# Summing the adaLN modulation by quarters of the partitions in a one-core decoder layer

## The chip, the core and the metric

The kernel runs on one core of one Trainium2 chip. The metric is the device time of one execution in microseconds (us), from the first to the last instruction with what lies around them; lower is better.

## The reference

One layer over a sequence of 256 tokens with 2048 channels, batch 1, all in float32: a SwiGLU FFN (hidden width 5632), a mixer of two parallel branches (causal pooling and windowed attention), and a second SwiGLU FFN. Each of the three is modulated by a vector c of 2048 numbers:

```python
mod = (jax.nn.silu(c) @ w_ada[l] + b_ada[l]).reshape(B, 3 * N_SUB, 1, D)

h = modulate(rms_norm(x, g_ffn1[l]), mod[:, 0], mod[:, 1])
x = x + 0.5 * mod[:, 2] * swiglu(h, w_ffn1_gu[l], w_ffn1_down[l])
...
```

So there are nine modulation vectors of 2048 numbers. For each sub-layer i, vector 3i is a shift, 3i + 1 a scale and 3i + 2 a gate on the residual. w_ada is 2048 by 18432, 151 MB, 16.8 MB for each vector. The product with one row silu(c) has so little arithmetic per weight that the kernel gives it to VectorE.

## The kernel before

**The large products.** TensorE multiplies activations by weights in float32r. For accuracy both are split into a high part (ScalarE's cast, L285) and the rest (VectorE's subtraction, L289), and three products are added: hi by hi, lo by hi, hi by lo (`mm`, L292 to L304). A `Set` is a block of output columns, at most 1024 wide, over all slices k of 128 rows of a weight matrix; it holds four PSUM banks (two token tiles by two chunks of 512). One slice k of a set is one *turn*: 2 token tiles by 3 terms by 2 chunks, 12 matmuls of 128x128 by 512 columns. Weights come as tiles named raw of 1 MB, two slices at a time, by one DMA each on SP's queue (`load`, L258 to L262). There are six raw buffers, shared with the modulation's weights.

**The order.** It is written out by hand. `push` (L106) issues the splitting of a slice two turns ahead (LAG) of its matmuls; `at(n, f)` (L116) puts extra work into turn n; `hop(n, f, g)` (L124) puts a small product into turn n and its use into the next, away from the ends of sets. A planner keeps an account of VectorE's time per turn: `room` is what a turn has (ROOM, 2.6 us for a full turn), `busy` what is booked by `will(n, t)`; `spread(n0, m, cost, cap)` (L143) puts m pieces of work of a given cost into the first turns with room, at most `cap` us of them a turn. In the two FFN calls the cap is ROWS.

**The modulation.** Vectors 0 and 1 come first, on a path of their own (`ada_load`, `ada_acc`, `ada_col`, L650 to L672 and L804 to L823), which the change leaves as it is apart from the shape of its column of ones. The other seven go through `ada_plan` (L180 to L237). For a block of 1024 (or, twice for vector 7, 512) outputs, 16 slices of w_ada are loaded, each 128 rows on the 128 partitions; VectorE multiplies a slice by the 128 numbers of silu(c) that belong to it (cs, one per partition) and adds it to an accumulator acc (L228, L230). Then acc must be summed over the partitions, in chunks of 512 outputs (`sums`): acc is split in two float32r halves (L189, L190), TensorE multiplies both by a 128x128 matrix of ones (L195, L196), and every partition then has every sum. For a gate that is the form wanted, and ScalarE copies it to `gates` (L202). For a shift or scale the numbers are wanted in columns, channel by partition: `mod_col` multiplies by the identity (L168), reduces (L171), and adds the biases (L175 to L178).

**Which vectors run where.** Vectors 2, 4, 3 and the first 512 outputs of 7 run in the second half of the first FFN (the `ffn` call at L902); 5, 6 and the rest of 7 in the mixer (L1180); 8 in the second FFN (L1261). Gate 2 is used when the first FFN's output is added to x (L420), gate 5 in the mixer's output projection, gate 8 at the end.

**The mixer's attention** copies the outputs of two heads from PSUM with VectorE (L1166) and books 0.8 us for them. It loads its bias tables on POOL's queue (L1138).

Of the kernel before, what the change touches and what calls it, by code (L numbers as in the profile page):

```python
# [9 lines left out]
F32 = mybir.dt.float32  # L10
F32R = mybir.dt.float32r
# [5 lines left out]
P = 128  # L17
# [16 lines left out]
RAW = 6  # L34
# [2 lines left out]
NS = 7  # L37
LAG = 2
ROOM = 2.6
ROWS = 1.3  # L40


@with_exitstack
def trunk_layer(ctx, tc, x, c, w_ada, b_ada, g_ffn1, w_ffn1_gu, w_ffn1_down, g_mix, w_in,
# [10 lines left out]
    def nm(s):  # L55
        uid[0] += 1
        return f"{s}_{uid[0]}"

    def t_(shape, tag, bufs=1, dt=F32):
        return sb.tile(list(shape), dt, tag=tag, bufs=bufs, name=nm(tag))  # L60
# [16 lines left out]

    ident = const.tile([P, P], F32, name="ident")
    make_identity(nc, ident)
    ones_f = const.tile([P, P], F32, name="ones_f")  # L80
    nc.gpsimd.memset(ones_f, 1.0)
    ones = const.tile([P, P], F32R, name="ones")
    nc.vector.tensor_copy(ones, ones_f)

    x_sb = const.tile([P, T, D], F32, name="x_sb")

# [29 lines left out]
    def at(n, f, first=False):  # L116

        fs = plan.setdefault(max(n, done[0]), [])
        fs.insert(0, f) if first else fs.append(f)
# [35 lines left out]
    def will(n, t):  # L155
        busy[n] = busy.get(n, 0.0) + t

    ada_v = w_ada[0].rearrange("(k p) n -> p k n", p=P)  # L160
    mcol = const.tile([P, 9, KD], F32, name="mcol")
    gates = {}

    def mod_col(j, b, c0):

        k, n = c0 // P, b.shape[1] // P
        d = t_([P, n, P], "t2", T2)
        nc.vector.tensor_tensor(d, b.rearrange("p (a q) -> p a q", a=n),  # L168
                                ident.unsqueeze(1).to_broadcast([P, n, P]), ALU.mult)
        m = mcol[:, j, k:k + n]  # L170
        nc.vector.tensor_reduce(m, d, AX.X, ALU.add)  # L171
        i, o = j // 3, j % 3
        bc = bcol[:, (2 * i + o) * KD + k:(2 * i + o) * KD + k + n]
        if o == 0:
            nc.vector.tensor_tensor(m, m, bc, ALU.add)  # L175
        else:
            nc.vector.scalar_tensor_tensor(out=m, in0=m, scalar=1.0, in1=bc, op0=ALU.add, op1=ALU.add)
            nc.vector.tensor_tensor(m, m, gcol[:, i * KD + k:i * KD + k + n], ALU.mult)  # L178

    def ada_plan(js, n0, cap=9.0):  # L180

        def sums(j, c0, a, n, o):
            got = []

            def halves():
                hi, lo = t_([P, CW], "t2", T2, F32R), t_([P, CW], "t2", T2, F32R)
                nc.scalar.copy(hi, a[0][:, o:o + CW])  # L189
                nc.vector.tensor_tensor(lo, a[0][:, o:o + CW], hi.bitcast(F32), ALU.subtract)  # L190
                got.extend((hi, lo))

            def prod():
                got.append(bank())
                nc.tensor.matmul(got[2], ones, got[0], start=True, stop=False)  # L195
                nc.tensor.matmul(got[2], ones, got[1], start=False, stop=True)  # L196

            def use():
                if j % 3 == 2:
                    if j not in gates:  # L200
                        gates[j] = t_([P, D], "gate", 1)
                    nc.scalar.activation(gates[j][:, c0 + o:c0 + o + CW], got[2], AF.Copy, scale=1.0 if j == 5 else 0.5)  # L202
                else:
                    mod_col(j, got[2], c0 + o)

            at(n, halves)
            q = hop(n + 2, prod, use, 2)
            will(n, 0.65)
            if j % 3 != 2:
                will(q + 1, 1.7)  # L210
            return q

        for j, c0, a_w in js:
            a, r, nk = [], [], 2 * SW // a_w
            where = spread(n0, KD, 1.24 * a_w / SW, cap)
            for kk, n in enumerate(where):
                def go(j=j, c0=c0, kk=kk, a=a, r=r, w=a_w, nk=nk):
                    if kk == 0:
                        a.append(t_([P, w], "acc", 2))
                        if j % 3 == 2:  # L220
                            nc.gpsimd.memset(a[0], 0.0)
                            nc.gpsimd.dma_start(a[0][0:1, :], b_ada[0:1, j * D + c0:j * D + c0 + w])
                    if kk % nk == 0:
                        r[:] = [t_([P, nk, w], "raw", RAW)]
                        nc.sync.dma_start(r[0], ada_v[:, kk:kk + nk, j * D + c0:j * D + c0 + w])
                    sc = cs[:, kk:kk + 1]
                    if kk == 0 and j % 3 != 2:
                        nc.vector.tensor_scalar_mul(a[0], r[0][:, 0, :], sc)  # L228
                    else:
                        nc.vector.scalar_tensor_tensor(out=a[0], in0=r[0][:, kk % nk, :], scalar=sc, in1=a[0],  # L230
                                                       op0=ALU.mult, op1=ALU.add)
                at(n, go)
                will(n, 1.24 * a_w / SW)
            n0 = n
            q = n
            for i in range(a_w // CW):
                q = sums(j, c0, a, max(n + 1 + 2 * i, q + 1), i * CW)  # L237


    class Set:  # L240
# [406 lines left out]

    at(16, small_things)

    def ada_load(c0, w, k0):  # L650
        nk = SW // w
        raw = t_([P, nk, 2, w], "raw", RAW)
        for j in (1, 0):
            nc.sync.dma_start(raw[:, :, j, :], ada_v[:, k0:k0 + nk, j * D + c0:j * D + c0 + w])  # L654
        return raw
# [103 lines left out]
    for j in (1, 0):  # L759
        for kk in (13, 14, 15):  # L760
            ada_acc(acc0[:, j], braw[3][:, kk - 12, j], kk, False)
        first_pe(12, j)
        for a in range(2):
            nc.tensor.matmul(bsum[j][a], acc0[:, j, a * P:(a + 1) * P], ones_f[:, 0:1], start=False, stop=True)
        if j:
            b8 = x_T(xr[1], bank_at(6, (P, 2, S)))
    nc.vector.tensor_copy(gcol, b[:, :KG])
# [37 lines left out]
    for k, n, need in ((2, 4, 14), (6, 4, 42), (10, 4, 70), (14, 2, 74)):  # L805
        nk = SW // (n * P)
        acc, raw, cost = [], [], 1.28 * n / 4

        def rows(kk, k=k, n=n, nk=nk, acc=acc, raw=raw):
            if kk == 0:  # L810
                acc.append(t_([P, 2, n * P], "acc", 2))
            if kk % nk == 0:
                raw[:] = [ada_load(k * P, n * P, kk)]
            ada_acc(acc[0], raw[0][:, kk % nk], kk, kk == 0)

        def end(k=k, n=n, acc=acc):
            b = bank((P, 2, n))
            for j in (1, 0):
                for a in range(n):
                    nc.tensor.matmul(b[:, j, a:a + 1], acc[0][:, j, a * P:(a + 1) * P], ones_f[:, 0:1],  # L820
                                     start=True, stop=True)
            for j in (1, 0):
                ada_col(k, n, j, b[:, j, :])  # L823

        where = [kk * 12 // KD for kk in range(KD)] if k == 2 else spread(max(e, 14), KD, cost)
        for kk in range(KD):
            at(where[kk], lambda rows=rows, kk=kk: rows(kk))
            will(where[kk], cost)
        e = where[-1] + (2 if k > 6 else 1)
        assert e + 1 < need, (k, e, need)  # L830
        will(e, 0.4)
        will(e + 1, 0.65 * n // 2)
        at(e, end)

        q = k
        while q < k + n:
            m = 1 if q == k + n - 1 else 2
            if q - q % 2 in xT:
                at(e + (q > k + 1), lambda q=q, m=m: h_pair(xT[q - q % 2][:, q % 2:q % 2 + m, :], q, m))
            else:  # L840
                xn, o = [], (q - k) // 2
                at(e - 1 + o, lambda q=q, xn=xn, m=m: xn.append(x_row(q, m)))
                n_ = e + 1 + o
                while n_ in ends or n_ - 1 in ends:
                    n_ += 1
                at(n_, lambda q=q, xn=xn, m=m: h_pair(x_T(xn[0], bank((P, m, S))), q, m))
            q += m
# [47 lines left out]
    def toe_out():  # L895
# [4 lines left out]

    hop(pushed[0] + 8, toe_prod, toe_out)
    s = ffn(w_ffn1_gu[0], w_ffn1_down[0], hh, hl, actT, NS // 2 * SW, part[NS - 1], None, 2, sumsq,  # L902
            [(j, c, SW) for j in (2, 4, 3) for c in (0, SW)] + [(7, 0, CW)])


    WI = w_in[0]
# [177 lines left out]
    def heads(n, g):  # L1084
# [78 lines left out]

        for blk in range(2):
            with_bank(n + 8, (P, 2, P), out_prod(blk),
                      lambda b, blk=blk: nc.vector.tensor_copy(attnT[:, g - 1:g + 1, blk * P:(blk + 1) * P], b), 1)  # L1166
        will(n + 9, 0.8)

    for half_ in range(2):
        for q in range(2):  # L1170
# [6 lines left out]
        will(W1 - 1 + 2 * q, 1.4)  # L1177
    for g, n in enumerate((2, 5, 9, 13, 17, 22, 25, 28)):
        heads(G[0] + n, g)
    ada_plan([(j, c, SW) for j in (5, 6) for c in (0, SW)] + [(7, CW, CW), (7, SW, SW)], nQ)  # L1180

    tk = [(t, i) for t in range(T) for i in range(2)]

# [74 lines left out]

    g, hh, hl = transition(s, SW, 5, 6, lambda stat: Set(w_ffn2_gu[0], KD, (0, SW), stat, flip=False, late=True))
    actT = t_([P, KF, S], "big", 1)  # L1260
    s = ffn(w_ffn2_gu[0], w_ffn2_down[0], hh, hl, actT, 0, None, g, 8, store, [(8, 0, SW), (8, SW, SW)])  # L1261
    flush()
    items = last_items(s, *new_h())

# [71 lines left out]
```

## Time and profile before

| | |
|---|---|
| three runs | 1994.84 us median (1994.56 to 1996.48) |
| the profiled execution | 1996.08 us, its span 1994.3 us |
| TensorE clock granted | 0.996 of full speed |
| DMA | 523.68 MB, mean 263 GB/s |

Here is the span in 40 slices of 50 us. The first FFN runs to about 767 us, the mixer to about 1263 us, the second FFN to the end. Each digit is the busy share of a slice in tenths; GB/s is what the DMA engines moved.

```profile
DVE  6898867989999978886889998888455454565655
ACT  6543457664664546446656455645564645565443
DMA  9989745899899966876688996598555645466652
GB/s 364 371 314 342 261 164 187 329 337 356 313 363 336 335 230 235 310 281 219 235 292 302 351 311 219 212 356 317 214 189 202 219 170 190 159 225 216 218 185 74
```

The stages in which `ada_plan` works stand out: DVE (VectorE) and DMA are at 8 to 9 tenths from 350 to 700 us, again over most of 800 to 1250 us, and from 1300 to 1400 us; elsewhere DMA is at 5 or 6.

In the rows, PE is TensorE's matmuls, PEld its weight loads, ACT ScalarE, POOL GpSimd, SP SyncE, which issues most DMAs. A matmul's duration is longer than the time between two of them, since they overlap; the pace is read from the chain.

### The profile page before, as it was taken

The page shows a single profiled execution, that of the slowest core. Times are in us where ns is not written, and L with a number is a line of the kernel's source. Part 1 is how long each engine was busy: PE and PEld are TensorE (multiplying, and loading weights), DVE is VectorE, ACT ScalarE, POOL GpSimd, SP SyncE. Part 2 cuts the span into 40 slices and gives each one's busy share as a digit, 9 for nine tenths or more (in the row PEclk, how much of TensorE's full clock was granted, in tenths as well). Part 3 has the DMA queues.
Part 4 walks back from the last instruction along what each step waited for, and adds up shares of the span by engine and source line. Part 5 has one row for each costly group of instructions (what it writes and reads, how often), then busy time and mean ns, then how long its engine had stood idle before and what let it go on. Part 6 is the DMA issues. An engine that isn't in the chain of part 4 may idle for free.

```text
span 1994.3 us, 23770 instructions
## 1 busy us (share of the span) xinstructions
PE 1972.3 (99%) x8873; PEld 1629.3 (82%) x8873; DVE 1513.6 (76%) x1749; ACT 1091.8 (55%) x1484; POOL 26.4 (1%) x51
## 2 busy tenths in 40 slices
PE   7999999999999999999999999999999999999999
PEld 6788888888788888888788888888888888888887
DVE  6898867989999978886889998888455454565655
ACT  6543457664664546446656455645564645565443
POOL 0000000000000000000000000000000000000000
PEclk9999999999999999999999999999999999999999
DMA  9989745899899966876688996598555645466652
GB/s 364 371 314 342 261 164 187 329 337 356 313 363 336 335 230 235 310 281 219 235 292 302 351 311 219 212 356 317 214 189 202 219 170 190 159 225 216 218 185 74
DMA packets 158212, 523.68 MB, mean 263 GB/s; under 512 B 9325, under 2 KB 21509, under 8 KB 157840
## 3 DMA queue, kind: packets, MB, share of 16 engines
q1 hardware_dynamic: 156464, 518.83, 72.7%
q0 software_dynamic: 1632, 3.34, 0.6%
q8 instruction: 69, 1.13, 0.2%
q14 instruction: 47, 0.39, 0.1%
HBM read 520.00 MB, written 2.12 MB: 262 GB/s over the span
## 4 chain that ended last, share of the span: by engine, by line
PE 96%; DVE 2%; DMA 1%; SPq 0%; issue 0%; ACT 0%; DVEq 0%; ACTq 0%
PE bank L304 93%; DVE acc L662 1%; DMA raw<-in_w_ffn_gu_dram 1%; DMA raw<-in_w_ada_dram 0%; DVE wl L289 0%; PE bank L1065 0%; SPq L654 0%; PE bank L820 0%; PE bank L196 0%; PE bank L195 0%; PE bank L357 0%; PE bank L1128 0%; PE bank L1092 0%; PE bank L999 0%; PE bank L1051 0%
## 5 line engine op out<-in xcount | busy, mean ns | idle before, releaser
L285 ACT CAST wh<-raw 128x1024 fp32r<-128x1024 f32 (+2 forms) x711 | 711.1, 1002 | 793.9 <-PE bank L304 739.7
L289 DVE TENSOR_TENSOR wl<-raw,wh 128x1024 fp32r<-128x1024 f32 (+2 forms) x713 | 823.5, 1157 | 418.4 <-ACT wh L285 413.7
L304 PE MATMUL bank<-wh,hl 128*128 128x512 f32 (+1 forms) x2088 | 653.6, 388 | 0.0
L304 PE MATMUL bank<-wh,hh 128*128 128x512 f32 (+1 forms) x2064 | 651.3, 390 | 0.3 <-DVE big L1099 0.3
L304 PE MATMUL bank<-wl,hh 128*128 128x512 f32 (+1 forms) x2064 | 647.5, 389 | 0.6 <-DVE wl L289 0.6
L304 PEld LDWEIGHTS bank<-wh,hl 128*128 128x128 f32 x2088 | 392.7, 188 | 81.3
L304 PEld LDWEIGHTS bank<-wl,hh 128*128 128x128 f32 x2064 | 388.2, 188 | 82.9 <-DVE wl L289 2.9
L304 PEld LDWEIGHTS bank<-wh,hh 128*128 128x128 f32 x2064 | 386.4, 189 | 80.2 <-issue 0.8
L230 DVE SCALAR_TENSOR_TENSOR acc<-raw,cs,acc 128x1024 f32<-128x1024 f32 (+1 forms) x231 | 279.8, 1211 | 0.8
L304 PE MATMUL bank<-wh,sh 128*128 128x512 f32 x656 | 203.7, 390 | 0.0
L304 PE MATMUL bank<-wh,sl 128*128 128x512 f32 x656 | 203.3, 389 | 0.0
L304 PE MATMUL bank<-wl,sh 128*128 128x512 f32 x656 | 203.1, 389 | 0.0
L304 PEld LDWEIGHTS bank<-wh,sl 128*128 128x128 f32 x656 | 123.0, 188 | 26.0 <-DVE sl L394 0.3
L304 PEld LDWEIGHTS bank<-wl,sh 128*128 128x128 f32 x656 | 123.1, 188 | 25.8
L304 PEld LDWEIGHTS bank<-wh,sh 128*128 128x128 f32 x656 | 122.6, 188 | 25.8 <-issue 0.4
L542 ACT COPY big<-raw 32x512 f32<-32x512 f32 (+1 forms) x208 | 121.9, 586 | 4.2
L662 DVE SCALAR_TENSOR_TENSOR acc<-raw,cs,acc 128x1024 f32<-128x1024 f32 (+2 forms) x74 | 77.7, 1052 | 1.0
L394 DVE TENSOR_TENSOR sl<-big,sh 128x512 fp32r<-128x512 f32 x82 | 56.2, 686 | 0.0
L393 ACT CAST sh<-big 128x512 fp32r<-128x512 f32 x82 | 50.7, 618 | 0.0
L784 DVE TENSOR_TENSOR big<-bank,big 128x512 f32<-128x512 f32 x56 | 36.4, 684 | 0.0
L329 ACT ACTIVATE junk<-x_sb 128x512 bf16<-128x512 f32 x24 | 15.2, 632 | 13.9 <-DVE x_sb L421 11.7
L538 DVE STREAM_TRANSPOSE raw<-sg 128x1024 f32<-128x1024 f32 (+1 forms) x20 | 22.7, 1133 | 0.0
(220 smaller groups left out, 802.7 us busy)
## 6 DMA issues: line engine op xcount, KB each, us to landing
raw<-in_w_ffn_gu_dram SPq DMA_DIRECT2D x175, 1024.0 KB, 5.3
raw<-in_w_ada_dram SPq DMA_DIRECT2D x112, 1024.0 KB, 7.2
raw<-in_w_ffn_down_dram SPq DMA_DIRECT2D x86, 1024.0 KB, 6.1
raw<-in_w_in_dram SPq DMA_DIRECT2D x48, 1024.0 KB, 6.8
raw<-in_w_ada_dram SPq DMA_DIRECT2D x64, 512.0 KB, 7.6
raw<-in_w_o_dram SPq DMA_DIRECT2D x15, 1024.0 KB, 7.8
raw<-in_w_pool_up_dram SPq DMA_DIRECT2D x8, 1024.0 KB, 7.9
raw<-in_w_attn_up_dram SPq DMA_DIRECT2D x8, 1024.0 KB, 6.9
```

The source lines that it names most:

```text
L230: nc.vector.scalar_tensor_tensor(out=a[0], in0=r[0][:, kk % nk, :], scalar=sc, in1=a[0], op0=ALU.mult, op1=ALU.add)
L285: nc.scalar.copy(wh, raw_k)
L289: nc.vector.tensor_tensor(wl[:, e], raw_k[:, e], wh[:, e].bitcast(F32), ALU.subtract)
L304: nc.tensor.matmul(self.banks[t][i], a[:, sl], w[:, o], start=first and q == 0, stop=last and q == 2)
L329: nc.scalar.activation(junk, x_sb[:, t, n * CW:(n + 1) * CW], AF.Square, scale=(D / 2) ** -0.5, accum_out=ssq[:, t, n:n + 1])
L393: nc.scalar.copy(hi, src[:, k:k + n, :])
L394: nc.vector.tensor_tensor(lo, src[:, k:k + n, :], hi.bitcast(F32), ALU.subtract)
L538: nc.vector.transpose(z[0][:, t, :], (src() if callable(src) else src)[:, t, 0:n])
L542: nc.scalar.copy(actT[32 * j:32 * j + 32, k:k + m, :].rearrange("p k (t i r) -> p k t i r", t=T, i=4)[:, :, :, i, :], z[0][32 * i:32 * i + ...
L662: nc.vector.scalar_tensor_tensor(out=acc, in0=r, scalar=sc, in1=acc, op0=ALU.mult, op1=ALU.add)
L784: nc.vector.tensor_tensor(a, b, a, ALU.add)
```

## The change

- A new view of w_ada: a tile of 128 partitions now holds, in each quarter q of 32 partitions, 32 rows of w_ada for the outputs 512q to 512q + 511. One accumulator of 128x512 serves a whole vector of 2048 outputs. A vector takes 64 accumulations of 128x512 (one for each group of 32 rows) where it took 32 of 128x1024.
- A raw tile (four groups of 32 rows) is loaded by four DMAs of 256 KB, each to 32 partitions, in runs of 2 KB.
- silu(c) is laid out anew to match (cs4), by 16 small ScalarE copies between turns 80 and 92.
- Shifts and scales (4, 3, 7, 6): the accumulator's four 128x128 blocks are the float32 weights, and the moving operand is `ind`, four columns, column q being 1 on quarter q's partitions. The result is the vector in columns at once; there are no halves and no `mod_col`.
- Gates (2, 5, 8): the halves are taken once for the whole vector, multiplied with `ind` as the weights, which gives four rows of 512; these are scaled, written to DRAM on POOL's queue, and read back to all 128 partitions.
- The planner: 0.75 us a row of 512; ROWS is 1.5, not 1.3; vector 7 is split at 24 of 64 rows instead of at a quarter of its columns; in the mixer the rest of 7 comes first, then 5 and 6.
- The attention's output copies go to ScalarE, and their 0.8 us are no longer booked.

```diff
-ROWS = 1.3
+ROWS = 1.5
...
+    ind = const.tile([P, 4], F32, name="ind")
+    nc.gpsimd.memset(ind, 0.0)
+    for q in range(4):
+        nc.gpsimd.memset(ind[32 * q:32 * q + 32, q:q + 1], 1.0)
...
+    ada_q = w_ada[0].rearrange("(m r) n -> r m n", r=32)
...
+            def row_prod():
+                got.append(bank())
+                nc.tensor.matmul(got[2][0:4, :], indr, got[0], start=True, stop=False)
+                nc.tensor.matmul(got[2][0:4, :], indr, got[1], start=False, stop=True)
+
+            def row_use():
+                nc.scalar.activation(a[0][0:4, :], got[2][0:4, :], AF.Copy, scale=1.0 if j == 5 else 0.5)
+                row = dram.tile([1, D], F32, name=nm("row"))
+                nc.gpsimd.dma_start(row[0].rearrange("(q n) -> q n", q=4), a[0][0:4, :])
+                gates[j] = t_([P, D], "gate", 1)
+                nc.gpsimd.dma_start(gates[j], row[0:1, :].to_broadcast([P, D]))
+
+            def col_prod():
+                got.append(bank((P, 4, 4)))
+                for c_ in range(4):
+                    nc.tensor.matmul(got[0][:, c_, :], a[0][:, c_ * P:(c_ + 1) * P], ind, start=True, stop=True)
+
+            if j % 3 == 2:
+                at(n + 1, halves)
+                will(n + 1, 0.65)
+                return hop(n + 3, row_prod, row_use, 2)
+            q = hop(n + 1, col_prod, lambda: mod_cols(j, got[0]), 2)
+            will(q + 1, 0.3)
             return q
...
+                    if m % 4 == 0:
+                        raw[:] = [t_([P, 4, CW], "raw", RAW)]
+                        for q in range(4):
+                            o = j * D + q * CW
+                            nc.sync.dma_start(raw[0][32 * q:32 * q + 32], ada_q[:, m:m + 4, o:o + CW])
...
-            [(j, c, SW) for j in (2, 4, 3) for c in (0, SW)] + [(7, 0, CW)])
+            [(j, 0, MR) for j in (2, 4, 3)] + [(7, 0, MR * 3 // 8)])
...
-                      lambda b, blk=blk: nc.vector.tensor_copy(attnT[:, g - 1:g + 1, blk * P:(blk + 1) * P], b), 1)
-        will(n + 9, 0.8)
+                      lambda b, blk=blk: nc.scalar.copy(attnT[:, g - 1:g + 1, blk * P:(blk + 1) * P], b), 1)
...
-    ada_plan([(j, c, SW) for j in (5, 6) for c in (0, SW)] + [(7, CW, CW), (7, SW, SW)], nQ)
+    ada_plan([(7, MR * 3 // 8, MR), (5, 0, MR), (6, 0, MR)], nQ)
```

More of the change, by code (lines that the diff above doesn't have):

```diff
@@ L79, in trunk_layer @@
     make_identity(nc, ident)
-    ones_f = const.tile([P, P], F32, name="ones_f")
+    ones_f = const.tile([P, 1], F32, name="ones_f")
     nc.gpsimd.memset(ones_f, 1.0)
-    ones = const.tile([P, P], F32R, name="ones")
-    nc.vector.tensor_copy(ones, ones_f)
+    ind = const.tile([P, 4], F32, name="ind")
+    nc.gpsimd.memset(ind, 0.0)
+    for q in range(4):
+        nc.gpsimd.memset(ind[32 * q:32 * q + 32, q:q + 1], 1.0)
+    indr = const.tile([P, 4], F32R, name="indr")
     x_sb = const.tile([P, T, D], F32, name="x_sb")
@@ L160, in trunk_layer @@
     ada_v = w_ada[0].rearrange("(k p) n -> p k n", p=P)
+    ada_q = w_ada[0].rearrange("(m r) n -> r m n", r=32)
     mcol = const.tile([P, 9, KD], F32, name="mcol")
[L162 to L171, printed above, removed]
+    cs4 = const.tile([P, KD, 4], F32, name="cs4")
@@ L172, in mod_col, with mod_cols @@
+    MR = D // 32
+    gates, part_sums = {}, {}
+    def mod_cols(j, b):
+        byq = lambda a: a.rearrange("p (q a) -> p q a", q=4)
+        m, s = byq(mcol[:, j, :]), b.rearrange("p a q -> p q a")
         i, o = j // 3, j % 3
-        bc = bcol[:, (2 * i + o) * KD + k:(2 * i + o) * KD + k + n]
+        bc = byq(bcol[:, (2 * i + o) * KD:(2 * i + o + 1) * KD])
         if o == 0:
-            nc.vector.tensor_tensor(m, m, bc, ALU.add)
+            nc.vector.tensor_tensor(m, s, bc, ALU.add)
         else:
-            nc.vector.scalar_tensor_tensor(out=m, in0=m, scalar=1.0, in1=bc, op0=ALU.add, op1=ALU.add)
-            nc.vector.tensor_tensor(m, m, gcol[:, i * KD + k:i * KD + k + n], ALU.mult)
+            nc.vector.scalar_tensor_tensor(out=m, in0=s, scalar=1.0, in1=bc, op0=ALU.add, op1=ALU.add)
+            nc.vector.tensor_tensor(m, m, byq(gcol[:, i * KD:(i + 1) * KD]), ALU.mult)
@@ L180, in ada_plan, with ends_of @@
     def ada_plan(js, n0, cap=9.0):
-        def sums(j, c0, a, n, o):
-            got = []
+        def ends_of(j, n):
+            a, got = part_sums[j], []
             def halves():
                 hi, lo = t_([P, CW], "t2", T2, F32R), t_([P, CW], "t2", T2, F32R)
-                nc.scalar.copy(hi, a[0][:, o:o + CW])
-                nc.vector.tensor_tensor(lo, a[0][:, o:o + CW], hi.bitcast(F32), ALU.subtract)
+                nc.scalar.copy(hi, a[0])
+                nc.vector.tensor_tensor(lo, a[0], hi.bitcast(F32), ALU.subtract)
@@ L191, in halves @@
                 got.extend((hi, lo))
-            def prod():
+            def row_prod():
                 got.append(bank())
[L195 to L210, printed above, removed]
-            return q
[L213 to L219, printed above, removed]
+                nc.tensor.matmul(got[2][0:4, :], indr, got[0], start=True, stop=False)
@@ L220, in go @@
+        raw = []
+        for j, m0, m1 in js:
+            a = part_sums.setdefault(j, [])
+            for m, n in zip(range(m0, m1), spread(n0, m1 - m0, 0.75, cap)):
+                def go(j=j, m=m, a=a):
+                    if m == 0:
+                        a.append(t_([P, CW], "acc", 2))
                         if j % 3 == 2:
                             nc.gpsimd.memset(a[0], 0.0)
[L222 to L225, printed above, removed]
@@ L226, in go @@
-                    sc = cs[:, kk:kk + 1]
-                    if kk == 0 and j % 3 != 2:
-                        nc.vector.tensor_scalar_mul(a[0], r[0][:, 0, :], sc)
+                            for q in range(4):
+                                o = j * D + q * CW
+                                nc.gpsimd.dma_start(a[0][32 * q:32 * q + 1, :], b_ada[0:1, o:o + CW])
+                    if m % 4 == 0:
+                        raw[:] = [t_([P, 4, CW], "raw", RAW)]
+                        for q in range(4):
+                            o = j * D + q * CW
+                            nc.sync.dma_start(raw[0][32 * q:32 * q + 32], ada_q[:, m:m + 4, o:o + CW])
@@ L229, in go @@
+                    sc = cs4[:, m // 4, m % 4:m % 4 + 1]
+                    if m == 0 and j % 3 != 2:
+                        nc.vector.tensor_scalar_mul(a[0], raw[0][:, 0, :], sc)
                     else:
-                        nc.vector.scalar_tensor_tensor(out=a[0], in0=r[0][:, kk % nk, :], scalar=sc, in1=a[0],
+                        nc.vector.scalar_tensor_tensor(out=a[0], in0=raw[0][:, m % 4, :], scalar=sc, in1=a[0],
                                                        op0=ALU.mult, op1=ALU.add)
@@ L232, in ada_plan @@
                 at(n, go)
-                will(n, 1.24 * a_w / SW)
+                will(n, 0.75)
             n0 = n
-            q = n
-            for i in range(a_w // CW):
-                q = sums(j, c0, a, max(n + 1 + 2 * i, q + 1), i * CW)
+            if m1 == MR:
+                ends_of(j, n)
     class Set:
@@ L648, in trunk_layer, with quarter_cs @@
     at(16, small_things)
+    def quarter_cs(s):
+        for q in range(4):
+            nc.scalar.copy(cs4[32 * q:32 * q + 32, :, s], cs[32 * s:32 * s + 32, :])
+    at(80, lambda: nc.vector.tensor_copy(indr, ind))
+    for s in range(4):
+        at(80 + 4 * s, lambda s=s: quarter_cs(s))
     def ada_load(c0, w, k0):
@@ L763, in trunk_layer @@
         for a in range(2):
-            nc.tensor.matmul(bsum[j][a], acc0[:, j, a * P:(a + 1) * P], ones_f[:, 0:1], start=False, stop=True)
+            nc.tensor.matmul(bsum[j][a], acc0[:, j, a * P:(a + 1) * P], ones_f, start=False, stop=True)
         if j:
@@ L819, in end @@
                 for a in range(n):
-                    nc.tensor.matmul(b[:, j, a:a + 1], acc[0][:, j, a * P:(a + 1) * P], ones_f[:, 0:1],
+                    nc.tensor.matmul(b[:, j, a:a + 1], acc[0][:, j, a * P:(a + 1) * P], ones_f,
                                      start=True, stop=True)
@@ L1260, in trunk_layer @@
     actT = t_([P, KF, S], "big", 1)
-    s = ffn(w_ffn2_gu[0], w_ffn2_down[0], hh, hl, actT, 0, None, g, 8, store, [(8, 0, SW), (8, SW, SW)])
+    s = ffn(w_ffn2_gu[0], w_ffn2_down[0], hh, hl, actT, 0, None, g, 8, store, [(8, 0, MR)])
     flush()
```

## The prediction

> **What bounds the kernel now.** I read the page's first table first, then the chain that ended last, then the chain and the waits cut to the stages in which the modulation sums run, and last the groups, windows and DMA rows of the work that the change touches.
>
> ```profile
> PE 1972.3 (99%) x8873; PEld 1629.3 (82%) x8873; DVE 1513.6 (76%) x1749; ACT 1091.8 (55%) x1484; POOL 26.4 (1%) x51
> PE 96%; DVE 2%; DMA 1%; SPq 0%; issue 0%; ACT 0%; DVEq 0%; ACTq 0%
> ...
> 415.04 0.23 PE bank L195
> 415.27 0.24 PE bank L196
> 415.51 8.20 PE bank L304 x36
> ```
>
> TensorE is busy 99% of the span and holds 96% of the chain. The last three lines (the chain around 415 us) show its pace: 36 of the large products in 8.20 us, 0.228 us each, so a turn of twelve (one slice k of a 1024-wide set) takes 2.73 us. The two products of the old sums, L195 and L196, stand on that same chain with 0.47 us a pair. Whatever TensorE gains or loses in issue time is gained or lost at the end; the other engines count only where they make it wait.
>
> How much does it wait where the modulation runs? The waits of the weight loader, first in 500 to 762 us, then in 770 to 1262 us:
>
> ```profile
> PEld bank L304 <- DVE wl L289: 1.4, 3, 0.7
> PEld bank L196 <- DVE t L190: 0.4, 1, 0.4
> ...
> PEld bank L304 <- DVE wl L289: 0.7, 2, 0.6
> ```
>
> That is 2.5 us for VectorE in all. So the most that a lighter VectorE can give back is about 2.5 us of 1994.
>
> **TensorE's own work.** The change removes the ones-products of 28 chunks of 512 outputs and puts back one pair for each of the vectors 2, 5 and 8. Removed: 25 pairs by 0.47 us = 11.8 us. Added: each of the vectors 4, 3, 7 and 6 gets four products, with one 128x128 block of the accumulator as the float32 weights and the four indicator columns moving. The nearest rows are those of the first modulation, where an accumulator block is also the weights and one column of ones moves:
>
> ```profile
> L820 PE MATMUL bank<-ones_f,acc 128*128 128x1 f32 x56 | 7.0, 254 | 1.5 <-DVE acc L662 1.5
> ...
> 128.30 1.68 PE bank L820 x16
> 129.98 2.20 PE bank L304 x9
> ```
>
> The code issues 28 such products (2 vectors by 4+4+4+2 blocks) and the trace has 56: a float32 product runs as two passes. On the chain 16 passes, the eight products of one block of four, take 1.68 us: 0.105 us a pass, 0.21 us a product. Four columns instead of one should not show beside the weight load. So 16 products by 0.21 = 3.4 us. The bounds are 1.7 us (one pass each) and about 7 us (each batch of four pays once more for the change from the large products and back); I take 3.4, because that row has the same types and the same kind of weights and its 1.68 us holds such a change. TensorE's sum: 3.4 - 11.8 = **-8.4 us**, all of it on the chain.
>
> **VectorE.** These rows carry its sum:
>
> ```profile
> L289 DVE TENSOR_TENSOR wl<-raw,wh 128x1024 fp32r<-128x1024 f32 x633 | 774.0, 1223 | 392.3 <-ACT wh L285 389.8 <-ACT wh L266 0.5
> L230 DVE SCALAR_TENSOR_TENSOR acc<-raw,cs,acc 128x1024 f32<-128x1024 f32 x201 | 257.3, 1280 | 0.3
> L230 DVE SCALAR_TENSOR_TENSOR acc<-raw,cs,acc 128x512 f32<-128x512 f32 x30 | 22.5, 750 | 0.5
> L228 DVE TENSOR_SCALAR acc<-raw,cs 128x1024 f32<-128x1024 f32 x7 | 5.2, 749 | 0.0
> L190 DVE TENSOR_TENSOR t<-acc,t 128x512 fp32r<-128x512 f32 x28 | 19.2, 686 | 1.3 <-ACT t L189 1.2
> L168 DVE TENSOR_TENSOR t<-bank,ident 128x512 f32<-128x512 f32 x16 | 11.0, 685 | 0.0
> L171 DVE TENSOR_REDUCE mcol<-t 128x4 f32<-128x512 f32 x16 | 11.0, 686 | 0.6
> L1166 DVE COPY big<-bank 128x256 f32<-128x256 f32 x8 | 3.0, 419 | 0.0
> ```
>
> Before, accumulating takes 257.3 + 22.5 + 5.2 = 285 us (two first rows of 512 left out). After, it is 7 vectors by 64 rows = 448 instructions by 0.750 us = 336 us, a little less for the four first ones: +50 us. Taken away: 25 subtractions of L190 (17.2 us), L168 and L171 (22.0 us), some 2.5 us of small column operations, and the eight copies L1166 that go to ScalarE (8 by 0.419 = 3.4 us): -45 us. VectorE ends about 5 us heavier in 1514, spread over 900 us. What goes is bunched, though: L168, L171 and the halves come in clumps of some 2 us in one or two turns, and those made the waits above. I credit the 2.1 us in which those waits fell within the chunk sums' own stage (the first stage's 1.4 + 0.4, and half of the mixer's 0.7).
>
> Against it stand new waits. A column product now follows one turn after the last accumulation, not two turns after it by way of the halves. If VectorE is late there, TensorE waits for one accumulation, up to 1.5 us, at each of four places: 0 to 6 us, and behind that wait stand the large products of the next turn. I take 1 us, since VectorE prepares weights two turns ahead and the waits above are few. With ROWS at 1.5 the cap no longer binds in the gate/up turns: 2.6 - 1.18 leaves 1.42 us a turn, 1.9 rows. With the 1.22 us that a weight split takes this makes 2.64 us of a 2.73 us turn, tight but under it. In the half-width turns (1.37 us) it is 0.69 + 0.71 = 1.40 us, 0.03 us over in 32 turns: 1 us. Three eighths of vector 7 instead of a quarter in the first FFN is 0.125 by 48 us = 6 us more for VectorE there, which the room at its end takes.
>
> **ScalarE, the gates, POOL, SP.** ScalarE loses 9 copies L202 of 0.59 us and 25 casts of the same size, and gains the eight copies and 16 small ones for the re-laid c: lighter by over 10 us at 55% busy, so nothing. A gate row now goes out to DRAM and comes back to 128 partitions on POOL's queue:
>
> ```profile
> out_dram<-x_sb POOLq DMA_DIRECT2D x4, 256.0 KB, 5.1
> toe<-sl POOLq DMA_DIRECT2D x1, 24.0 KB, 5.7
> raw<-in_w_ada_dram SPq DMA_DIRECT2D x112, 1024.0 KB, 7.2
> L225 SPq DMA_DIRECT2D raw<-in_w_ada_dram x112: 367/368/422, 340.7 to 1378.4; - x112
> SPq L225 <- DVE wl L289: 176.9, 57, 7.7
> SPq L225 <- DVE acc L230: 128.7, 44, 5.8
> L420 DVE TENSOR_TENSOR t<-bank,gate x20: 683/684/692, 646.6 to 1885.2; 128x512 f32<-128x512 f32 x20
> L230 DVE SCALAR_TENSOR_TENSOR acc<-raw,cs,acc x92: 744/1280/1291, 804.6 to 1208.9; 128x1024 f32<-128x1024 f32 x77, 128x512 f32<-128x512 f32 x15
> L420 DVE TENSOR_TENSOR t<-bank,gate x4: 683/684/686, 1219.6 to 1236.4; 128x512 f32<-128x512 f32 x4
> L202 ACT ACTIVATE gate<-bank x12: 576/592/613, 415.6 to 1415.6; 128x512 f32<-128x512 f32 x12
> ```
>
> Two such trips are 5.7 + about 7 us, 13 us in all. The last lines (the two of L230 and L420 with fewer records are the mixer's alone) show when a gate is made and when it is used: the first gate at 416 us against 647 us, the last by 1416 us against uses that end at 1885 us. Gate 5 moves behind the rest of vector 7: 104 of the mixer's 168 rows then stand up to its end, and 62% of the way from 805 to 1209 us is 1055 us, against a first use at 1220 us. The trips are hidden; the bias loads of the heads queue behind them on POOL by 13 us at most, a few turns before a head needs its bias. They would cost up to 13 us if a gate came last. SP issues four loads for each MB instead of one, 4 by 0.368 = 1.47 us, and the next weight load stands 1.1 us later behind them. SP mostly waits for buffers (the L225 lines: 306 us for 112 loads), so I take nothing.
>
> **The loads themselves** are the cost that no row shows. The bytes stay: 112 MB of w_ada. Runs of 2 KB are not the problem: between 50 and 100 us, where the first modulation reads runs of 2 KB, the chip moved 372 GB/s. But every load that row counts goes to all 128 partitions, and now each quarter goes to 32.
>
> ```profile
> core 0: us, PE busy (x) PEld busy (x) DVE busy (x) ACT busy (x) POOL busy (x), PEclk, DMA share, GB/s
> 50.00:100.00 50.00, 48.49 (x207) 39.68 (x206) 42.28 (x42) 27.90 (x38) 4.52 (x11) 0.93 1.01 372
> 350.00:700.00 350.00, 349.73 (x1534) 286.99 (x1533) 319.90 (x334) 204.21 (x269) 1.95 (x3) 1.00 0.92 339
> 800.00:1250.00 450.00, 449.35 (x2122) 370.28 (x2121) 386.65 (x522) 251.63 (x392) 8.80 (x12) 1.00 0.79 282
> 1300.00:1400.00 100.00, 100.00 (x442) 82.75 (x441) 87.56 (x77) 51.23 (x59) 0.00 (x0) 1.00 0.92 341
> ```
>
> Where the sums run, the 16 DMA engines are 92%, 79% and 92% busy. At 339 GB/s and 0.92, a busy set moves 368 GB/s, so a tile of 1.05 MB takes 2.85 us. Let a quarter-wise tile take f times that. The first FFN loads 54 such tiles (3.375 vectors by 16) and has 0.08 by 350 = 28 us of idle DMA time, so up to f = 1.18 nothing shows. Ends: f = 1, nothing; f = 2, if four quarters in a row each reach only half of the ways into the memory. At f = 1.5 the first FFN is short by 77 - 28 = 49 us; the mixer (42 tiles, 60 us, idle 94 us) by nothing; the second FFN (16 tiles, 23 us, idle 8 us) by 15 us: **+64 us**. At f = 2 it is 126 + 26 + 38 = +190 us. For the forecast I take f = 1, the value of every row there is, and keep the rest as a rival.
>
> Sum: -8.4 - 2.1 + 1 + 1 = **-8.5 us** on the profiled execution's 1996.08 us (span 1994.3), which lies 1.2 us above the median of 1994.84. Brought to the median: 1986.3 us.
>
> **Rivals.** (1) *Quarter loads fill the DMA engines for longer* (slower than before). Place: the first FFN, then the first 100 us of the second. Point: f above 1.18 costs, and from about f = 1.22 it has eaten the 8.5 us. Price: +64 us at f = 1.5, so 2050 us; 2000 to 2176 us over f = 1.25 to 2. For it: a DMA share of 0.92, only six load tiles in flight, and TensorE at 99%, which leaves nowhere to catch up. Against it: no row shows a narrow load slow. [...] (2) *VectorE overflows at the higher cap* (no change): if waits for wl fill 0.1 us of each of the 100 fullest turns, 10 us come back and 1996 us follow. It decides from 0.04 us a turn on, where the gain falls within the measurement. For it: 2.64 of 2.73 us. Against it: the planner's sums leave room, and VectorE ran at 91% from 350 to 700 us (319.90 of 350) with 2 us of waits.
>
> **How the numbers follow.** A measurement of this kernel can tell about 0.2%, 4 us, from no change. The forecast (1982 to 1991 us on its own, from the bounds of the small products and of the new waits) gets 0.48, rival 1 0.42, rival 2 0.10. Of the forecast's 0.48, 0.46 lie more than 4 us below before and 0.02 within. Of rival 1's 0.42, 0.01, 0.04 and 0.37 are faster, same and slower, the first two at f near 1.2. Of rival 2's 0.10, 0.02, 0.07 and 0.01. Faster: 0.49. Same: 0.13. Slower: 0.38. So faster is likelier and close together, slower is a little less likely and spread over 170 us. The range runs from 1981 us to 2075 us (rival 1 up to about f = 1.6); what lies above, some 0.17, is left out.
>
> **What would show it.** The two float32r products of a gate's rows with three records each, and the column products with 32 records at about 0.105 us on the chain: TensorE's sum. No L168 and L171, and accumulations of 0.75 us: VectorE's. A DMA share near 1 between 350 and 700 us at fewer GB/s than 339, ScalarE's casts or the accumulations waiting for raw, and the longer landing of w_ada would show rival 1 and make the forecast wrong. Waits of the weight loader for wl beyond 5 us would show rival 2.

## The result and the profile after

| | before | changed |
|---|---|---|
| median | 1994.74 us (1994.56 to 1996.48, 4 runs) | 2189.6 us (2187.14 to 2214.82, 4 runs) |
| ratio to before | | 1.1003, 95% interval 1.0922 to 1.1084 |
| profiled execution, span | 1996.08, 1994.3 us | 2187.14, 2185.4 us |

The change makes the kernel 195 us, 10%, slower. The page of the changed kernel, busy times and chain (its large products are L316, where before has L304):

```profile
PE 2039.4 (93%) x8855; PEld 1638.6 (75%) x8855; DVE 1514.0 (69%) x1874; ACT 1069.9 (49%) x1474; POOL 28.5 (1%) x65
PE 58%; DMA 30%; DVE 7%; issue 2%; ACT 2%; SPq 0%; DVEq 0%; ACTq 0%
PE bank L316 56%; DMA raw<-in_w_ada_dram 15%; DMA raw<-in_w_ffn_down_dram 6%; DMA raw<-in_w_ffn_gu_dram 5%; DVE wl L301 3%; DMA raw<-in_w_in_dram 2%; ACT wh L297 1%; DVE acc L243 1%; DMA raw<-in_w_attn_up_dram 1%; DMA raw<-in_w_pool_up_dram 1%; DMA raw<-in_w_o_dram 0%; DVE acc L682 0%; PE bank L1085 0%; DVE sl L406 0%; SPq L238 0%
```

DMA has 30% of the chain where it had 1%. It is not w_ada alone (15%): the weights of the FFNs and of the mixer, whose loads the change does not touch, have another 15%; they are issued on the same queue, in turn with it. The windows in which the sums run, the accumulations (the last figures are VectorE's idle time before them and what ended most of it, 0.3 us before the change), and the loads of w_ada with their landing time show the same:

```profile
350.00:700.00 350.00, 300.28 (x1191) 227.37 (x1190) 245.40 (x305) 155.09 (x209) 1.56 (x3) 0.95 0.96 260
800.00:1250.00 450.00, 427.30 (x1987) 346.21 (x1985) 350.42 (x540) 233.64 (x388) 12.00 (x20) 0.98 0.89 251
1300.00:1400.00 100.00, 87.66 (x366) 67.85 (x367) 75.13 (x93) 43.07 (x57) 0.00 (x0) 0.97 0.92 253
...
L243 DVE SCALAR_TENSOR_TENSOR acc<-raw,cs,acc 128x512 f32<-128x512 f32 x444 | 332.4, 749 | 76.3 <-DMA raw<-in_w_ada_dram 67.2
...
raw<-in_w_ada_dram SPq DMA_DIRECT2D x448, 256.0 KB, 11.8
```

The last two figures of a window are the DMA share and GB/s. The engines are busier than before in the first stage (0.96 against 0.92) and move less: 260 GB/s against 339. A load of a quarter of the bytes takes 11.8 us to land where the whole took 7.2. VectorE's busy time, 1514.0 us against 1513.6, has not moved.

Where the time came from, by stage: the rows that scale x stand at the start of the mixer (the first of them) and of the second FFN (the last of them, some 28 us into it). Before, changed, and the changed kernel with whole loads, which is the first experiment on the change below:

```profile
L350 DVE TENSOR_SCALAR t<-x_sb,st x16: 540/542/547, 765.1 to 1289.3; 128x512 f32<-128x512 f32 x16
```

```profile
L362 DVE TENSOR_SCALAR t<-x_sb,st x16: 540/543/548, 879.6 to 1455.9; 128x512 f32<-128x512 f32 x16
```

```profile
L361 DVE TENSOR_SCALAR t<-x_sb,st x16: 540/542/547, 757.3 to 1277.3; 128x512 f32<-128x512 f32 x16
```

Against the last, the changed kernel loses 122 us in the first FFN, 56 us in the mixer (576.3 against 520.0 from the first of these rows to the last) and 26 us in the rest of the span.

### The profile page after: what moved, and what is told of

The parts are those of the page before. It is cut to its first block, busy times and chain, and to the rows that moved or that the text cites. A ratio compares the mean times of both kernels' runs of the same rounds, so it can differ in the third digit from the quotient of the medians.

```text
span 2185.4 us, 24337 instructions
## 1 busy us (share of the span) xinstructions
PE 2039.4 (93%) x8855; PEld 1638.6 (75%) x8855; DVE 1514.0 (69%) x1874; ACT 1069.9 (49%) x1474; POOL 28.5 (1%) x65
## 4 chain that ended last, share of the span: by engine, by line
PE 58%; DMA 30%; DVE 7%; issue 2%; ACT 2%; SPq 0%; DVEq 0%; ACTq 0%
PE bank L316 56%; DMA raw<-in_w_ada_dram 15%; DMA raw<-in_w_ffn_down_dram 6%; DMA raw<-in_w_ffn_gu_dram 5%; DVE wl L301 3%; DMA raw<-in_w_in_dram 2%; ACT wh L297 1%; DVE acc L243 1%; DMA raw<-in_w_attn_up_dram 1%; DMA raw<-in_w_pool_up_dram 1%; DMA raw<-in_w_o_dram 0%; DVE acc L682 0%; PE bank L1085 0%; DVE sl L406 0%; SPq L238 0%
## 5 line engine op out<-in xcount | busy, mean ns | idle before, releaser
L316 PE MATMUL bank<-wh,hh 128*128 128x512 f32 (+1 forms) x2064 | 665.2, 398 | 53.7 <-ACT wh L297 50.8
L316 PE MATMUL bank<-wl,hh 128*128 128x512 f32 (+1 forms) x2064 | 661.4, 396 | 26.9 <-DVE wl L301 25.3
L316 PE MATMUL bank<-wh,hl 128*128 128x512 f32 (+1 forms) x2088 | 662.3, 393 | 1.8 <-DVE hl L406 1.8
L316 PEld LDWEIGHTS bank<-wh,hh 128*128 128x128 f32 x2064 | 389.5, 191 | 148.1 <-ACT wh L297 65.4
L316 PEld LDWEIGHTS bank<-wl,hh 128*128 128x128 f32 x2064 | 389.8, 191 | 128.6 <-DVE wl L301 50.2
L316 PEld LDWEIGHTS bank<-wh,hl 128*128 128x128 f32 x2088 | 397.4, 190 | 87.0 <-DVE hl L406 3.1
L243 DVE SCALAR_TENSOR_TENSOR acc<-raw,cs,acc 128x512 f32<-128x512 f32 x444 | 332.4, 749 | 76.3 <-DMA raw<-in_w_ada_dram 67.2
L316 PE MATMUL bank<-wh,sh 128*128 128x512 f32 x656 | 210.6, 401 | 19.5 <-ACT sh L405 19.3
L316 PE MATMUL bank<-wh,sl 128*128 128x512 f32 x656 | 209.9, 400 | 11.3 <-DVE sl L406 11.1
L316 PE MATMUL bank<-wl,sh 128*128 128x512 f32 x656 | 207.5, 396 | 1.4 <-DVE wl L301 1.4
L316 PEld LDWEIGHTS bank<-wh,sh 128*128 128x128 f32 x656 | 124.3, 193 | 52.2 <-ACT sh L405 26.6
L316 PEld LDWEIGHTS bank<-wh,sl 128*128 128x128 f32 x656 | 123.9, 192 | 46.4 <-DVE sl L406 21.4
L316 PEld LDWEIGHTS bank<-wl,sh 128*128 128x128 f32 x656 | 125.4, 191 | 29.6 <-DVE wl L301 2.7
## 6 DMA issues: line engine op xcount, KB each, us to landing
raw<-in_w_ada_dram SPq DMA_DIRECT2D x448, 256.0 KB, 11.8
```

Of the source, the lines that this page charges most:

```text
L243: nc.vector.scalar_tensor_tensor(out=a[0], in0=raw[0][:, m % 4, :], scalar=sc, in1=a[0], op0=ALU.mult, op1=ALU.add)
L316: nc.tensor.matmul(self.banks[t][i], a[:, sl], w[:, o], start=first and q == 0, stop=last and q == 2)
```

## The experiments

**On the kernel before: what makes a load slow.** Four kernels change nothing but how the plan's 1 MB load of w_ada is issued; all compute the whole layer. The slices of the second and the third are shown against the first, the quarters. Theory 1 is the prediction's first rival (neighbouring partitions); the ways into the memory that its expectations speak of are the author's supposition. The others are that the number and size of the DMAs (2), the short runs (3) or the new plan of the sums (4) are to blame.

*Quarters of 32 neighbours.*

```diff
-nc.sync.dma_start(r[0], ada_v[:, kk:kk + nk, j * D + c0:j * D + c0 + w])
+for q in range(4):
+    e = slice(32 * q, 32 * q + 32)
+    nc.sync.dma_start(r[0][e], ada_v[e, kk:kk + nk, j * D + c0:j * D + c0 + w])
```

> The kernel before with one change: each load of w_ada in the plan (1 MB, 128 partitions) is issued as four loads, one to each 32 neighbouring partitions. Theory 1 (a load to 32 neighbouring partitions reaches half of the ways into the memory, f about 2): 2150 to 2200 us, and from 350 to 700 us a DMA share above 0.95 at 250 to 265 GB/s. Theory 2 (four small DMAs cost more than one, whatever partitions they go to): the same here, 2150 to 2200 us. Theory 3 (the runs of 2 KB or the columns read side by side are slow) and theory 4 (the new plan of the sums is slow): 1995 us plus or minus 4, since runs and plan are those of before.

Measured: 2219.11 us, ratio 1.1115 (1.1083 to 1.1147). The old plan with its old runs loses as much as the change and a little more, so theories 3 and 4 fall as its main cause. The time lies above the range that was expected, and the rate just below it. The window from 350 to 700 us:

```profile
350.00:700.00 350.00, 298.11 (x1139) 225.04 (x1138) 236.31 (x247) 153.95 (x212) 1.95 (x3) 0.93 0.97 248
```

*Quarters of every fourth partition.*

```diff
-    e = slice(32 * q, 32 * q + 32)
+    e = slice(q, P, 4)
```

> The kernel before with each load of w_ada in the plan issued as four loads of 32 partitions, but load q goes to every fourth partition (q, q+4, ... q+124) instead of 32 neighbours. Count, size and runs are those of the run with neighbouring quarters. Theory 1 (which partitions decide): 1995 to 2030 us, a DMA share near 0.92 at about 335 GB/s from 350 to 700 us. Theory 2 (number and size of DMAs): 2150 to 2200 us. Theories 3 and 4: 1995 us plus or minus 4.

Measured: 1999.35 us, ratio 1.0021 (1.0010 to 1.0032). Same number of loads, same size, same runs, other partitions, and 220 us are gone; some 4 us above before remain:

```profile
350.00:700.00 350.00, 344.78 (x1505) 282.33 (x1504) 313.29 (x326) 200.26 (x265) 1.95 (x3) 1.00 0.91 334
```

The share and the rate are those of before again. Theory 2 falls.

*Halves of 64 neighbours.*

```diff
-for q in range(4):
-    e = slice(32 * q, 32 * q + 32)
+for q in range(2):
+    e = slice(64 * q, 64 * q + 64)
```

> The kernel before with each load of w_ada in the plan issued as two loads, one to each 64 neighbouring partitions. Theory 1 (the first 64 partitions share the same ways as the first 32): 2150 to 2200 us, as with quarters. Theory 2 (a fixed cost for each DMA): half of the extra DMAs or fewer, so 2040 to 2100 us. Theories 3 and 4: 1995 us plus or minus 4.

Measured: 2230.41 us, ratio 1.1172 (1.1139 to 1.1204). Twice as many partitions to a load, half as many loads, and at least as slow as the quarters (2219.11 us), as theory 1 alone had it. The time is again above the range.

*Four pieces to all 128 partitions.*

```diff
-nc.sync.dma_start(r[0], ada_v[:, kk:kk + nk, j * D + c0:j * D + c0 + w])
+for i in range(nk):
+    for o in range(0, w, nk * CW // 2 if w > CW else CW):
+        nc.sync.dma_start(r[0][:, i, o:o + CW],
+                          ada_v[:, kk + i, j * D + c0 + o:j * D + c0 + o + CW])
```

> The kernel before with each load of w_ada in the plan issued as four loads of 256 KB, each to all 128 partitions (one row, 512 columns, runs of 2 KB). Count and size are those of the quarters, and the runs are as short as in the changed kernel. Theory 1: 1995 us plus or minus 4. Theory 2: 2150 to 2200 us. Theory 3 (short runs): slower than 2010 us.

Measured: 1996.53 us, ratio 1.0007 (0.9996 to 1.0019). Loads of 256 KB in runs of 2 KB cost the kernel before nothing that can be told.

**The price by itself.** A kernel that only loads w_ada, six ways in a row, and leaves out the layer; it ran once.

```diff
+for i in range(24):
+    raw = tile_()
+    nc.sync.dma_start(raw, src(i))
+    done(raw, i)
+for i in range(24, 48):
+    raw = tile_()
+    for q in range(4):
+        nc.sync.dma_start(raw[32 * q:32 * q + 32], src(i)[32 * q:32 * q + 32])
+    done(raw, i)
...
```

> The loads alone: all of w_ada in 144 tiles of 1 MB through the six buffers, a copy of four numbers a tile on VectorE, and x stored as the output (the whole layer is left out). Six stretches of 24 tiles: whole tiles; four loads of 32 neighbouring partitions; four of every fourth partition; two of 64 neighbours; eight of 16 neighbours; and whole tiles in turn with four of 32 neighbours. Theory 1 (neighbouring partitions share ways): at full rate about 360 GB/s for whole tiles and every fourth partition, 190 to 220 for 32 and for 64 neighbours alike, 100 to 110 for 16 neighbours, 250 to 270 for the mixture. A rival in which the number of partitions decides: 64 neighbours about 360 or at least half as slow again as 32. A rival in which a load's fixed time decides: every fourth partition as slow as 32 neighbours.

Its windows, one in each stretch (DVE and POOL are the only engines in it; the last two figures are DMA share and GB/s):

```profile
core 0: us, DVE busy (x) POOL busy (x), PEclk, DMA share, GB/s
30.00:80.00 50.00, 3.07 (x18) 0.00 (x0) 1.00 1.05 387
100.00:200.00 100.00, 3.40 (x20) 0.00 (x0) 1.00 1.07 212
220.00:260.00 40.00, 2.38 (x14) 0.00 (x0) 1.00 1.05 387
280.00:380.00 100.00, 3.57 (x21) 0.00 (x0) 1.00 1.06 218
400.00:560.00 160.00, 3.75 (x22) 0.00 (x0) 1.00 1.08 144
580.00:660.00 80.00, 3.40 (x20) 0.00 (x0) 1.00 1.06 267
```

In order: whole tiles 387 GB/s, 32 neighbours 212, every fourth partition 387, 64 neighbours 218, 16 neighbours 144, whole tiles in turn with quarters 267. So f, the prediction's factor, is 387 / 212 = 1.83 in a stream of loads alone. Whole tiles and every fourth partition (about 360 expected) and 16 neighbours (100 to 110 expected) came out faster than expected, the rest within their ranges. For the mixture, half of the bytes at 387 and half at 212 GB/s would give 274, beside 267 measured: here a narrow load delays those behind it by little more than its own time. The share is 1.05 to 1.08 in all six, at 144 to 387 GB/s, so it does not tell how fast the bytes move.

**On the change: what the rest of it is worth.** *Whole loads.* The same bytes of w_ada, but a tile is four row slices of 512 columns in one load to all 128 partitions. The weights then meet the wrong numbers of c, so this kernel leaves out a right modulation.

```diff
-for q in range(4):
-    o = j * D + q * CW
-    nc.sync.dma_start(raw[0][32 * q:32 * q + 32], ada_q[:, m:m + 4, o:o + CW])
+k, o = m // 16 * 4, j * D + m // 4 % 4 * CW
+nc.sync.dma_start(raw[0], ada_v[:, k:k + 4, o:o + CW])
```

> The changed kernel with each tile loaded by one DMA to all 128 partitions (four row slices of 512 columns, all bytes of w_ada once). The weights meet the wrong numbers of c, so this leaves out a right modulation; every instruction and every byte is otherwise that of the change. Theory 1 (the narrow loads are the whole loss and the rest of the change is worth what the prediction's sum says, TensorE -8.4 us and the waits about 0): 8.5 us below before, 1985 to 1989 us. Rival (VectorE overflows at the higher cap): within 4 us of before, with over 8 us of waits for wl.

Measured: 1982.62 us beside 1995.44 us, ratio 0.9935 (0.9922 to 0.9947). With the loads alone put right the change gains 12.8 us (10.6 to 15.6), so the whole of the loss lies in the loads; the time lies below the 1985 to 1989 us expected. Its waits of the weight loader, and its groups and chain pieces for the new products:

```profile
PEld bank L315 <- DVE wl L300: 0.7, 2, 0.3
```

```profile
L212 PE MATMUL bank<-ind,acc 128*128 128x4 f32 x32 | 4.0, 249 | 0.0
L200 PE MATMUL bank<-t,indr 128*4 128x512 f32 x3 | 1.2, 397 | 0.0
L199 PE MATMUL bank<-t,indr 128*4 128x512 f32 x3 | 1.2, 397 | 0.0
...
463.60 0.23 PE bank L199
463.83 0.23 PE bank L200
576.54 0.79 PE bank L212 x8
```

VectorE makes the weight loader wait 0.7 us over the whole run: the second rival falls.

*Every fourth partition, by row groups.* The first of two kernels with fast loads that compute the whole layer. Partition 4r + q holds row r for quarter q; the indicator columns are made from the identity, and silu(c) is spread by four small products.

```diff
-ada_q = w_ada[0].rearrange("(m r) n -> r m n", r=32)
+ada_q = w_ada[0].rearrange("(m r) (g q n) -> r g q m n", r=32, q=4, n=CW)
...
-nc.gpsimd.memset(ind, 0.0)
-for q in range(4):
-    nc.gpsimd.memset(ind[32 * q:32 * q + 32, q:q + 1], 1.0)
+nc.vector.tensor_reduce(ind, ident.rearrange("p (r q) -> p q r", q=4), AX.X, ALU.add)
...
+for i in range(4):
+    nc.sync.dma_start(raw[0][:, i, :], ada_q[:, j, :, m + i, :])
```

> The changed kernel with quarter q on partitions q, q+4, ... q+124 instead of 32 neighbours, and a tile loaded as four DMAs of one row group each: 256 KB, all 128 partitions, runs of 2 KB. The indicator columns and the laid-out c follow. Theory 1: about 8 us below before, 1985 to 1990 us. Rival (VectorE overflows): within 4 us of before. If four loads a tile cost by themselves: above 2050 us, though the kernel before with its loads in four pieces speaks against that.

Measured: 1988.78 us, ratio 0.9969 (0.9957 to 0.9981): 6.2 us below before, faster than both kernels.

*Every fourth partition, by quarters.* The same, with `nc.sync.dma_start(raw[0][q::4], ada_q[:, m:m + 4, o:o + CW])` for each q: the source is word for word that of the changed kernel.

> The same layout (quarter q on every fourth partition), but each quarter loaded by its own DMA of 256 KB to those 32 partitions, as the changed kernel does with neighbours. Theory 1: 1985 to 1995 us, since each load reaches all ways; the kernel before lost 3 us in this form. If 32 partitions are slow wherever they lie: about 2190 us.

Measured: 1988.95 us, ratio 0.9968 (0.9956 to 0.9979). In the earlier pairs the rows read from DRAM moved together with the partitions written. Here number, size, runs and source of the loads are those of the changed kernel and only the partitions written differ (with the small tables and the bias load that follow them), and 200 us are gone: it is the destination that decides. Theory 1's shared ways into the memory are one account of it; no trace shows them.

*The quarters in another order.* The changed kernel with `for q in (0, 2, 1, 3)`.

> The changed kernel with the four quarter loads of a tile issued in the order 0, 2, 1, 3. If loads that follow each other and go to different halves of the partitions run side by side, the ways of both halves are in use and most of the loss goes: 1990 to 2060 us. If the DMA engines go through the loads in step, one load at a time, so that half of the ways stand idle whatever the order: 2180 to 2200 us, as with the order 0, 1, 2, 3.

Measured: 2155.32 us, ratio 1.0799 (1.0775 to 1.0824). Neither number: 34 us of 195 come back, and from 350 to 700 us the chip moves 270 GB/s where it moved 260 in the other order. Here alternating between the halves helps, but only a little.

**Where half of the 12.8 us went.** *Four pieces of the whole loads.* Like the whole loads, this leaves out a right modulation.

```diff
+for i in range(4):
+    nc.sync.dma_start(raw[0][:, i, :], ada_v[:, k + i, o:o + CW])
```

> The changed kernel with each tile loaded in four DMAs of 256 KB to all 128 partitions, from the same places of w_ada as in the run with whole tiles (so the weights again meet the wrong numbers of c, which leaves out a right modulation). Between whole tiles (12.8 us below before) and row groups (6.6 us below): if SP's four issues a tile are the 6 us, 6 to 8 us below before, with a weight load late behind them at the start of the sums near 350 us; if the interleaved layout's reads are, 11 to 14 us below.

Measured: 1986.71 us, ratio 0.9959 (0.9947 to 0.9970), 8.2 us below before. By the medians the four issues take most of the difference and the layout the rest, but the intervals of neighbouring steps touch. In the kernel with row groups the chain passes at the start of the sums through SP's issues (L233) to a weight load that stands behind them:

```profile
355.51 8.04 DMA raw<-in_w_ffn_gu_dram
...
365.99 0.54 SPq L233
366.53 0.05 issue
366.58 0.60 SPq L233
367.18 0.05 issue
367.23 0.59 SPq L233
367.82 0.04 issue
367.87 0.60 SPq L233
...
368.56 7.77 DMA raw<-in_w_ffn_gu_dram
```

*ROWS back at 1.3.*

```diff
-ROWS = 1.5
+ROWS = 1.3
```

> The kernel with quarters on every fourth partition, loaded by row groups, with ROWS back at 1.3. If the pile of loads when the sums start (near 355 us) is the loss, fewer rows a turn thin it out: 9 to 11 us below before. If it is the four issues as such: 6 to 7 us below, as with 1.5.

Measured: 1994.81 us, ratio 0.9998 (0.9989 to 1.0007). Both expectations miss; the gain is gone. The rows of the sums no longer fit into the first FFN's turns, and what is left over is done at its end, in one piece, ahead of the last weights (the timeline of VectorE, and TensorE's wait):

```profile
744.47 10.20 DVE L238 SCALAR_TENSOR_TENSOR acc<-raw,cs,acc 128x512 f32<-128x512 f32 x13
```

```profile
PE bank L311 <- DVE wl L450: 5.2, 1, 5.2
```

*The loads on POOL's queue.* `nc.gpsimd.dma_start` in place of `nc.sync.dma_start` for the row groups.

> The same kernel at ROWS 1.5 with the row-group loads issued on POOL's queue, which is idle, so that SP has weight loads alone. If SP's issue time is the loss: 10 to 13 us below before. If POOL's own time for a load (0.73 us for the bias tables) or its later landing counts: 0 to 6 us below, or slower, with accumulations waiting for raw.

Measured: 2003.99 us, ratio 1.0037 (1.0024 to 1.0050): slower than before, as the second expectation allowed. The accumulations wait for their tiles, and TensorE for VectorE behind them:

```profile
DVE acc L238 <- DMA raw<-in_w_ada_dram: 20.6, 5, 8.2
PEld bank L311 <- DVE wl L296: 12.0, 9, 4.4
```

## Why the prediction was wrong

- **The step that failed** is "for the forecast I take f = 1, the value of every row there is". It is 1.83 by the loads alone. The kernels agree: all loads together keep the hardware queue busy for 79.0% of 2185.4 us in the changed kernel and 74.0% of 1980.8 us with whole loads, by the pages' queue rows:

```profile
q1 hardware_dynamic: 188464, 518.85, 79.0%
```

```profile
q1 hardware_dynamic: 183088, 518.83, 74.0%
```

  That is 1726 and 1466 us; the 260 us between them, put down to w_ada's 112 tiles, are 2.3 us a tile on top of 2.85, f = 1.8. Absence of a slow row was no evidence: no load of that shape and size ran in the trace. The row on record that could have weighed more was the DMA share of 0.92: with 28 us of idle DMA time for 54 tiles the forecast could bear an extra 0.5 us a tile and no more.
- **Rival 1** was right, at its place and beyond. Its price was too low: at f = 1.83 its formula gives 54 by 2.37 = 128 us, less 28 of idle time, so 100 us in the first FFN, 99 - 94 = 5 us in the mixer and 38 - 8 = 30 us in the second FFN, 135 us. Measured are 122, 56 and 26, 205 us in all against whole loads. The mis-sized term is the mixer's: its 94 us of idle DMA time were counted as if all of it could be used. By the difference, 99 - 56 = 43 us of it served as cover. Within the changed kernel's mixer some stretches have a full share while others have idle DMA time:

```profile
1000.00:1050.00 50.00, 44.97 (x211) 37.01 (x210) 28.22 (x61) 21.81 (x44) 4.73 (x8) 0.93 0.69 216
1200.00:1250.00 50.00, 43.46 (x184) 33.28 (x182) 34.16 (x41) 22.62 (x30) 3.61 (x7) 1.00 1.05 281
```

  The author's reading is that, with six tiles in flight, idle time far before or after a crowded stretch was of little use. It is argued from such windows; no run shows it. The first FFN's 122 us against 100 fit the same reading, that little of its 28 idle us helped.
- **The ways into the memory** that the prediction has at f = 2, and theory 1 in the expectations, are shown by no run. The values of f at which rival 1 was priced, 1.25 to 2, were assumptions, which no row of before shows. What the loads alone show are rates by destination: 387 GB/s for all 128 partitions and for every fourth, 212 and 218 for 32 and 64 neighbours, so f = 1.83 and 1.78. The order of the halves gave back 34 of 195 us.
- **TensorE's sum** held: with whole loads the four products of a vector take 0.79 us on the chain at both places in the first FFN, and in the changed kernel 0.98 us in the mixer and 1.17 us in the second FFN, so 3.7 us for 16 against 3.4 (eight passes with one column stand at 0.79 us on the chain of before too, so four columns did not show); a gate's pair takes 0.46 us.
- **The rest** was -8.5 us by the sum and is -12.8 us (-10.6 to -15.6) with whole loads. The 2 us booked for new waits did not come: 0.7 us for wl are left where before had 2.9. Some 2 us more may lie in the first 200 us: the first modulation's products that start at 195.4 us in the profile of before stand between 192.3 and 193.2 us in the profiles of the change and of four of its variants (whole loads, row groups, quarters on every fourth partition, the other order), and between 192.4 and 195.9 us in the five with the old setup. Why they stand earlier is left open.
- **The step "SP mostly waits for buffers, so I take nothing"** was too generous. Four loads a tile cost some 4.7 us between the kernels with whole and with fourfold loads, with intervals that touch near 10.6 us below before. In the kernel before four pieces cost nothing that can be told, and four loads to every fourth partition some 4 us.
- **The gates by DRAM, the moved copies and the higher cap** cost nothing visible in the kernel with whole loads. Without the higher cap the plan overflows (the kernel with ROWS at 1.3), which the prediction did not see.

## What to carry to other kernels

When a layout splits a tile over groups of neighbouring partitions, cost the load before the arithmetic: here loads to 32 or 64 neighbours ran at 212 and 218 GB/s, 55 and 56% of the 387 of whole tiles, and the loads queued behind them paid too (15% of the changed kernel's chain). The same split with a stride (every fourth partition) cost some 4 to 6 us in the layer where neighbours cost some 200, so choose the layout by where the loads land. And where a shared resource is as busy as the DMA engines here (a share of 0.92), an operation that no row shows needs the price of its slow case in the forecast, not the price of its nearest row.

## What the runs showed of the hardware that was not expected

Sixteen neighbours ran at 144 GB/s, 37% of whole tiles (100 to 110 beside 360 had been expected), while 32 and 64 ran at 55 and 56%. The DMA share did not tell the rate: 387 and 144 GB/s both stood at a share of 1.05 to 1.08. TensorE's granted clock was lower where it starved: 0.95 from 350 to 700 us in the changed kernel, with TensorE busy 300 of 350 us, against 1.00 in the same window before.
